# The factor of the norms: two products with a constant matrix and Exp of Ln, in place of one-column products, Sqrt and a transposed spread

## Chip, core and metric

The kernel runs on one core of a Trainium2 chip. The metric is the device time of one execution in microseconds (us). Engines: TensorE (PE, its weight loads PEld), VectorE (DVE), ScalarE (ACT), GpSimd (POOL), and SyncE (SP), which issues DMAs, as GpSimd does.

## The reference, cut to what matters

One decoder layer over 2048 tokens with 1024 channels, all in float32. Three sub-layers follow each other, each as x + RMSNorm(f(RMSNorm(x))):

```python
def rms_norm(x, g):
    y = x * lax.rsqrt(jnp.mean(x * x, axis=-1, keepdims=True) + EPS)
    return y * g
...
# 1. mixer: z = h @ w_in (a, g, q, k, v, forget logits)
#    u = silu(layer_norm(causal_conv31(a * sigmoid(g))))            512 channels
#    att = causal attention, 8 heads of 64, with cumulative log-forget bias
#    y = concat(u, att) @ w_out
# 2. cross-attention of 4 heads into 256 memory tokens (themselves normed)
# 3. y = square(relu(h @ w_up)) @ w_down                            hidden 4096
```

The layer norm over the 512 conv channels subtracts the mean and multiplies by rsqrt(mean of squares + EPS) as well.

## The kernel before

**Layout and precision.** Activations stand transposed: channels on the 128 partitions, tokens along the free dimension, in chunks of 512 tokens (TC), eight tiles of 128 channels (KT). A float32 product is made of three products in the f32r format: each operand is split into a high part (a ScalarE copy that rounds) and a low part (a VectorE subtraction), `split` (L134), and `mm3` (L160) adds high x high, high x low and low x high in PSUM.

**A norm.** `square_sum` (L169) squares the eight channel tiles on ScalarE and adds them on VectorE into one tile `ss` of 128 partitions x 512 tokens. `token_mean` (L177) turns each block of 128 tokens of `ss` by an f32 product with a one-column vector of 1/1024, so that the mean of a token lies on that token's partition, one column for each block. `token_rstd` (L185) applies Sqrt(mean + EPS) on ScalarE and a reciprocal on VectorE, on 128 x 4 elements. `spread` (L193) brings the factor back to a row over tokens on all partitions with one transpose on TensorE for each block, into the one PSUM bank of tag "stat", from which VectorE multiplies. So it is done in `normed` (L288: x, four chunks, and memory with 256 tokens), `conv_norm` (L455: four chunks, whose mean over channels is one f32 product with a broadcast column of ones, L463), `residual` (L650: behind the mixer and behind the cross-attention, four chunks each), `mlp_out` (L906: chunks 0 to 2) and `finale` (L863: chunk 3, in two halves of 256 tokens). Two further uses of `token_mean` need no spread: the norm ahead of the cross-attention (`mix_out`, L664, uses the factor as a scale per token) and the one ahead of the MLP (`mlp_prep`, L785).

**Stages and order.** `run` (L978): `mix_in` for the first half of the tokens with memory and the norms of the other two chunks beside it; `mix_in` for the second half, and the MLPs of chunks 0, 1 and 2, each with side work beside it (`tail`: for each chunk attention, `mix_out`, cross-attention); the MLP of chunk 3 alone; `finale`. `mlp_out(c)` runs beside the first five hidden blocks of the next chunk's MLP; `mlp_prep(c+1)` beside the last block of the MLP of chunk c. `drive` (L956) steps a main and a side generator in turn by the costs that they yield, side costs against main costs by a ratio (r0, a1, m0, m1, m2), and deals the conv taps out by another (a0, b1, bm). A planner then orders each engine's instructions by priority and by its own estimate of times; the other constants of SCHED (L57) shift priorities: weights are issued ahead by hw, conv taps behind by hb, side and main by hs and hm. While `Engine.pinned` is set (the first stretch of the kernel), each instruction of ScalarE and VectorE stays in the order of the program.

**Buffers.** Every tile has a tag with a number of buffers (L43 on): of [128 x 512] tiles "ms" has four for the main work (squares, relu, the reads `x2r` of the residual in `mlp_out`, `r2b` and `ssy` of the finale), "bs" three for the side work; in PSUM "mm" has two banks for main products, "stat" one.

**Tables.** ScalarE's functions come in table sets. A load (ACT_TABLE_LOAD) is put ahead of an activation whose function isn't in the set that is loaded; Square, Copy and Relu never need one.

Of the kernel before, what the change touches and what calls it, by code (L numbers as in the profile page):

```python
# [11 lines left out]
F32R = mybir.dt.float32r  # L12
AF = mybir.ActivationFunctionType
# [43 lines left out]
SCHED = dict(hw=153, hb=124, hs=61, hm=42.2, r0=0.254, a0=0.346, a1=1.16, b1=0.186, m0=0.85, m1=0.986, m2=1.12,  # L57
             bm=0.102, y1=3.12, y2=2.3, y3=2.97, y4=1.95)
# [22 lines left out]
class Trunk:  # L81
# [103 lines left out]
    def token_rstd(self, ss, mean):  # L185

        n = ss.shape[1] // P
        r = self.st([P, 4], name="rstd")[:, :n]
        self.a.activation(r, self.token_mean(ss, mean), AF.Sqrt, bias=self.eps, scale=1.0)
        self.v.reciprocal(r, r)  # L190
        return r

    def spread(self, r):  # L193

        n = r.shape[1]
        ps = self.ps("stat")
        for t in range(n):
            self.nc.tensor.transpose(ps[:, t * P : (t + 1) * P], r[:, t : t + 1].to_broadcast([P, P]), self.ident)
        return ps[:, : n * P]

# [11 lines left out]
    def setup(self):  # L212
# [6 lines left out]
        self.mean_d, self.mean_c = ct([P, 1], "mean_d"), ct([P, 1], "mean_c")  # L219
        self.v.memset(self.mean_d, 1.0 / D)  # L220
        self.v.memset(self.mean_c, 1.0 / CCH)
# [9 lines left out]

        self.tri = ct([P, P], "tri")
        self.same, self.prior = [ct([NH * 8, NH * 8], n) for n in ("same", "prior")]
# [14 lines left out]

    def setup_late(self):
# [12 lines left out]
        n = NH * 8  # L262
        sel = lambda t, pattern, base, cm: nc.gpsimd.affine_select(
            out=t, in_=t, pattern=pattern, compare_op=ALU.is_ge, fill=0.0, base=base, channel_multiplier=cm)
        for t in (self.tri, self.same, self.prior):
            nc.gpsimd.memset(t, 1.0)
        sel(self.tri, [[1, P]], 0, -1)
        sel(self.prior, [[1, n]], -1, -1)
        for t in (self.same, self.prior):
            t = t.rearrange("p (h t) -> p h t", t=8)  # L270
            sel(t, [[-8, NH], [0, 8]], 0, 1)
            sel(t, [[8, NH], [0, 8]], 7, -1)
# [15 lines left out]
    def normed(self, xs, g, w, stag, out=None, tags=None):  # L288
# [5 lines left out]
        r = self.token_rstd(ss, self.mean_d)  # L294
        yield 1
        r = self.spread(r)
# [50 lines left out]
    def mix_in(self, h, ht, late, after):  # L347
# [15 lines left out]
        for b in range(2):  # L363
# [32 lines left out]
    def glu(self, h, t, ht):  # L396
# [58 lines left out]
    def conv_norm(self, a, tag):  # L455
# [6 lines left out]
        mu = self.ps("stat")  # L462
        self.nc.tensor.matmul(mu, self.ones[:, 0:1].to_broadcast([P, P]), tot, start=True, stop=True)  # L463
        ss = self.tile(tag, [P, TC], name="lss")
        for t in range(4):
            self.v.scalar_tensor_tensor(out=a[:, t], in0=mu, scalar=-1.0 / CCH, in1=a[:, t],
# [3 lines left out]
        r = self.token_rstd(ss, self.mean_c)  # L470
        yield SCHED["y4"]
        r = self.spread(r)
        for t in range(4):
            self.mul(a[:, t], a[:, t], r)
            self.a.activation(a[:, t], a[:, t], AF.Silu, bias=self.cvec[:, 2, t : t + 1],
                              scale=self.cvec[:, 1, t : t + 1])
            yield SCHED["y4"]

    def gate(self, h, z):

        nc = self.nc
        z, e, u, ln, cum = z
# [18 lines left out]
        if h == 1:  # L501
            nc.tensor.matmul(ps[:n, :1], self.same, self.tot[0], start=True, stop=False)
        nc.tensor.matmul(ps[:n, :1], self.prior, self.tot[h], start=h == 0, stop=True)
# [146 lines left out]
    def residual(self, ys, ss, xs, dst):  # L650

        r = self.token_rstd(ss, self.mean_d)
        yield 1.5
        r = self.spread(r)
# [9 lines left out]
    def mix_out(self, c, g):  # L664
# [27 lines left out]
        yield from self.residual(ys, ss, xs, self.d_x1[c])  # L692
# [12 lines left out]
    def cross(self, c, h2, sc, g):  # L705
# [75 lines left out]
        yield from self.residual(ys, ss, xs, self.d_x2[c])  # L781
# [81 lines left out]
    def finale(self, c, cur, ys, r4):  # L863
# [8 lines left out]
        def out(sl, ssy):  # L872
            r = self.spread(self.token_rstd(ssy, self.mean_d))
# [32 lines left out]
    def mlp_out(self, c):  # L906
        nc = self.nc
        ys, ssy = self.fin.pop(c)
        r = self.spread(self.token_rstd(ssy, self.mean_d))
# [198 lines left out]
```

## Time and profile before

| | us |
|---|---|
| median of three runs | 2823.07 |
| lowest and highest | 2816.79, 2825.55 |
| profiled execution, its own time | 2820.59 |
| its span, first to last instruction | 2818.8 |
| TensorE busy | 2745.9 (97%) |
| VectorE busy | 1962.6 (70%) |
| ScalarE busy | 1372.1 (49%) |
| GpSimd busy | 206.1 (7%) |
| mean granted clock of TensorE, as a share | 0.995 |

How to read it: the median is what a change is measured by; the busy times and all rows below come from the one profiled execution. Register, branch, semaphore and DMA-issuing instructions are not counted as busy. Products on TensorE overlap in the records, so that their lengths add up to more than the time that they take.

### The profile page before, as it was taken

How to read it: one execution, taken by the hardware profiler on the slowest of the kernel's cores; microseconds unless marked ns; L12 is line 12 of the kernel's file. 1: busy time of each engine (PE TensorE's matmuls, PEld its weight loads, DVE VectorE, ACT ScalarE, POOL GpSimd, SP SyncE). 2: the span in 40 equal slices, each digit the busy share in tenths (PEclk: the TensorE clock that was granted, in tenths of full speed). 3: DMA queues.
4: the chain of work that ended last, by engine and by line, in shares of the span. 5: the costliest groups of instructions: out<-in, count | busy, mean ns of one | idle time of the engine just before them, and what ended most of it. 6: DMA issues, size and time to landing. Idle time of an engine off the chain costs nothing.

```text
span 2818.8 us, 36129 instructions
## 1 busy us (share of the span) xinstructions
PE 2745.9 (97%) x13300; PEld 2255.2 (80%) x13300; DVE 1962.6 (70%) x3596; ACT 1372.1 (49%) x2171; POOL 206.1 (7%) x376
## 2 busy tenths in 40 slices
PE   7999999999999999999999999999999999999997
PEld 5889778887877888777878888778777888888886
DVE  7677876668785666787885766997875555844436
ACT  5224644346654435465654444665555445543332
POOL 0010300001110000021100001021100000000000
PEclk9999999999999999999999999999999999999999
DMA  5375645456543334455543435464524342442222
GB/s 171 117 239 161 168 135 173 141 159 198 163 145 113 135 127 146 142 171 150 156 130 123 146 114 172 128 192 140 153 97 143 131 150 77 140 136 97 92 96 83
DMA packets 141169, 398.26 MB, mean 141 GB/s; under 512 B 15264, under 2 KB 38048, under 8 KB 136128
## 3 DMA queue, kind: packets, MB, share of 16 engines
q1 hardware_dynamic: 100080, 262.40, 28.3%
q0 software_dynamic: 40912, 133.54, 16.0%
q8 instruction: 105, 1.72, 0.3%
q14 instruction: 72, 0.59, 0.1%
HBM read 330.68 MB, written 65.20 MB: 140 GB/s over the span
## 4 chain that ended last, share of the span: by engine, by line
PE 87%; DMA 5%; DVE 4%; issue 2%; ACT 2%; POOL 0%; SPq 0%; DVEq 0%; POOLq 0%; ACTq 0%
PE mm L166 20%; PE mm L165 20%; PE mm L167 20%; PE sc L167 4%; PE sc L165 4%; PE sc L166 4%; PE o L631 4%; PE pt L613 4%; PE sc L578 2%; PE sc L579 2%; DMA rb<-drs 1%; DMA ks<-dk 1%; DVE yacc L73 1%; DMA x2r<-dx 1%; PE stat L182 1%
## 5 line engine op out<-in xcount | busy, mean ns | idle before, releaser
L73 ACT CAST wh<-wr 128x1024 fp32r<-128x1024 f32 x282 | 296.3, 1051 | 664.8 <-PE mm L166 602.0
L165 PE MATMUL mm<-h,wh 128*128 128x512 f32 x1504 | 597.7, 398 | 3.4 <-ACT h L73 2.6
L167 PE MATMUL mm<-h,wl 128*128 128x512 f32 x1504 | 595.0, 396 | 0.0
L166 PE MATMUL mm<-h,wh 128*128 128x512 f32 x1504 | 592.9, 394 | 1.8 <-DVE h L73 1.8
L73 DVE TENSOR_TENSOR wl<-wr,wh 128x1024 fp32r<-128x1024 f32 x282 | 345.0, 1224 | 278.0 <-ACT wh L73 276.6
L165 PE MATMUL mm<-hid,wh 128*128 128x512 f32 x992 | 397.6, 401 | 0.9 <-DVE yacc L73 0.9
L167 PE MATMUL mm<-hid,wl 128*128 128x512 f32 x992 | 395.6, 399 | 0.0
L166 PE MATMUL mm<-hid,wh 128*128 128x512 f32 x992 | 394.2, 398 | 0.0
L73 DVE SCALAR_TENSOR_TENSOR acc<-cu,convw,acc 128x512 f32<-128x512 f32 x480 | 357.6, 747 | 5.8
L165 PEld LDWEIGHTS mm<-h,wh 128*128 128x128 f32 x1504 | 283.4, 189 | 62.1 <-ACT h L73 3.0
L166 PEld LDWEIGHTS mm<-h,wh 128*128 128x128 f32 x1504 | 283.3, 188 | 59.8 <-DVE h L73 3.3
L167 PEld LDWEIGHTS mm<-h,wl 128*128 128x128 f32 x1504 | 283.0, 188 | 59.2 <-issue 0.5
L73 DVE TENSOR_TENSOR yacc<-mm,yacc 128x512 f32<-128x512 f32 (+1 forms) x232 | 154.7, 668 | 154.5 <-PE mm L167 153.6
L73 ACT CAST pp<-pt 128x512 fp32r<-128x512 f32 (+1 forms) x288 | 158.9, 561 | 135.5 <-PE pt L613 123.2
L165 PEld LDWEIGHTS mm<-hid,wh 128*128 128x128 f32 x992 | 186.5, 188 | 43.9 <-DVE yacc L73 2.2
L167 PEld LDWEIGHTS mm<-hid,wl 128*128 128x128 f32 x992 | 186.5, 188 | 41.9 <-issue 0.2
L166 PEld LDWEIGHTS mm<-hid,wh 128*128 128x128 f32 x992 | 186.6, 188 | 40.2 <-issue 0.2
L73 DVE TENSOR_TENSOR pp<-pt,pp 128x512 fp32r<-128x512 f32 (+1 forms) x288 | 185.8, 655 | 43.3 <-ACT pp L73 41.6
L613 PE MATMUL pt<-ident,prow 128*128 128x128 f32 x1088 | 195.1, 274 | 0.7 <-ACT prow L73 0.7
L73 DVE CUSTOM_DVE_ANT_0 prow<-sc,bias 128x512 f32<-128x512 f32 (+3 forms) x288 | 166.7, 595 | 24.6 <-PE sc L579 19.0
L73 ACT ACTIVATE prow<-prow,mx 128x128 f32<-128x128 f32 (+15 forms) x128 | 154.3, 1205 | 57.5 <-DVE mx L73 56.8
L613 PEld LDWEIGHTS pt<-ident,prow 128*128 128x128 f32 x1088 | 139.7, 141 | 33.0 <-ACT prow L73 3.9
(242 smaller groups left out, 4427.6 us busy)
## 6 DMA issues: line engine op xcount, KB each, us to landing
wr<-in_w_up_dram SPq DMA_DIRECT2D x128, 512.0 KB, 3.4
wr<-in_w_down_dram SPq DMA_DIRECT2D x128, 512.0 KB, 3.5
wr<-in_w_in_dram SPq DMA_DIRECT2D x32, 512.0 KB, 4.0
q<-dq POOLq DMA_DIRECT2D x64, 256.0 KB, 6.0
wr<-in_w_out_dram SPq DMA_DIRECT2D x32, 512.0 KB, 3.5
dx<-y SPq DMA_DIRECT2D x16, 1024.0 KB, 4.4
bias<-dnc POOLq DMA_DIRECT2D x32, 512.0 KB, 5.1
x<-in_x_dram POOLq DMA_DIRECT2D x12, 1024.0 KB, 6.2
```

Source lines behind the costliest of these rows:

```text
L73: ins = op(*args, **kw)
L165: mm(ps, ah, bh, start=first and j == 0, stop=False)
L166: mm(ps, ah, bl, start=False, stop=False)
L167: mm(ps, al, bh, start=False, stop=last and j == n - 1)
L182: self.nc.tensor.matmul(ps[:, t : t + 1], ss[:, t * P : (t + 1) * P], mean, start=True, stop=True)
L578: nc.tensor.matmul(ps[:, :w], q[:, 0, qs], ks[:, k0 : k0 + w], start=True, stop=False)
L579: nc.tensor.matmul(ps[:, :w], q[:, 1, qs], ks[:, k0 : k0 + w], start=False, stop=True)
L613: nc.tensor.transpose(pt[:, at : at + P], prow[t][:, (k0 + k) * P : (k0 + k + 1) * P], self.ident)
L631: nc.tensor.matmul(o[:, :, q], v[:, g + k], pp[:, :, at + q.start : at + q.stop], start=g == 0 and k == 0 and (n == 0 or nk == 2), stop=g ...
```

## The change

`wide_mean` splits the tile of sums into a high and a low part and multiplies both by one constant 128 x 128 matrix, every element 1/1024, in two f32r products: the mean of every token then lies on all partitions at once. `wide_rstd` takes Ln(mean x scale + EPS) and Exp of -0.5 times that on ScalarE, in place in the tile of sums, from which the multiplications read it; the spread is gone from `normed`, `conv_norm`, `residual`, `mlp_out` and `finale`. The conv norm's mean over channels goes through `wide_mean` as well, with a factor of two in the scalar, since the matrix holds 1/1024. `token_rstd`, left for the norm ahead of the cross-attention, takes Ln and Exp too. One table set is loaded by an instruction of its own (`ln_exp`) at the start, behind the second Sigmoid of each gated unit and behind the last Silu of a conv norm; each Sigmoid and Silu is kept behind the ScalarE instruction that was traced before it. The masks `same` and `prior` of the forget gate are made in the gate's own buffer before each half's value products, no longer once at the start. Of the constants of SCHED hw, hb, r0, m2, bm and y4 have new values. Code that isn't shown does not change.

```diff
-SCHED = dict(hw=153, hb=124, hs=61, hm=42.2, r0=0.254, a0=0.346, a1=1.16, b1=0.186, m0=0.85, m1=0.986, m2=1.12,
-             bm=0.102, y1=3.12, y2=2.3, y3=2.97, y4=1.95)
+SCHED = dict(hw=162, hb=117, hs=61, hm=42.2, r0=0.297, a0=0.346, a1=1.16, b1=0.186, m0=0.85, m1=0.986, m2=1.08,
+             bm=0.0831, y1=3.12, y2=2.3, y3=2.97, y4=2.07)
...
 def token_rstd(self, ss, mean):
-        self.a.activation(r, self.token_mean(ss, mean), AF.Sqrt, bias=self.eps, scale=1.0)
-        self.v.reciprocal(r, r)
+        self.a.activation(r, self.token_mean(ss, mean), AF.Ln, bias=self.eps, scale=1.0)
+        self.a.activation(r, r, AF.Exp, scale=-0.5)
...
+    def wide_mean(self, x, tag):
+        w = x.shape[1]
+        hi, lo = [self.tile(tag, [P, w], F32R, "wm") for _ in range(2)]
+        self.split(hi, lo, x)
+        ps = self.ps("stat")[:, :w]
+        self.nc.tensor.matmul(ps, self.wide, hi, start=True, stop=False)
+        self.nc.tensor.matmul(ps, self.wide, lo, start=False, stop=True)
+        return ps
+
+    def wide_rstd(self, ss, tag, n=D):
+        r = ss
+        ps = self.wide_mean(ss, tag)
+        self.a.activation(r, ps, AF.Ln, bias=self.eps, scale=float(D // n))
+        self.a.activation(r, r, AF.Exp, scale=-0.5)
+        return r
...
 # setup
+        self.wide = ct([P, P], "wide", F32R)
+        self.a.activation(self.wide, self.mean_d[:, 0:1].to_broadcast([P, P]), AF.Copy, scale=1.0)
-        self.a.activation(self.st([P, 1], name="warm"), self.eps, AF.Sqrt)
+        self.ln_exp()
...
 # normed
-        r = self.token_rstd(ss, self.mean_d)
+        r = self.wide_rstd(ss, stag)
         yield 1
-        r = self.spread(r)
         yield 1
...
 # mix_in, at b == 0
-                buf = self.tile("ms", [P, 4 * 8 * NH + P], name="gate")
+                buf = self.tile("ms", [P, 6 * 8 * NH + P], name="gate")
+                zs += [buf[: NH * 8, 384 + 64 * j : 448 + 64 * j] for j in range(2)]
+                self.gate_masks(*zs[5:])
...
 # glu
-            self.a.activation(sig, ps, AF.Sigmoid)
+            self.tc.keep_in_program_order(self.a.activation(sig, ps, AF.Sigmoid))
+            if j == 1:
+                self.ln_exp()
...
 # conv_norm
-        mu = self.ps("stat")
-        self.nc.tensor.matmul(mu, self.ones[:, 0:1].to_broadcast([P, P]), tot, start=True, stop=True)
+        mu = self.wide_mean(tot, tag)
...
-        r = self.token_rstd(ss, self.mean_c)
+        r = self.wide_rstd(ss, tag, CCH)
         yield SCHED["y4"]
-        r = self.spread(r)
         for t in range(4):
             self.mul(a[:, t], a[:, t], r)
-            self.a.activation(a[:, t], a[:, t], AF.Silu, bias=self.cvec[:, 2, t : t + 1],
-                              scale=self.cvec[:, 1, t : t + 1])
+            self.tc.keep_in_program_order(self.a.activation(
+                a[:, t], a[:, t], AF.Silu, bias=self.cvec[:, 2, t : t + 1], scale=self.cvec[:, 1, t : t + 1]))
+            if t == 3:
+                self.ln_exp()
...
 # residual
-        r = self.token_rstd(ss, self.mean_d)
+        r = self.wide_rstd(ss, tag)
         yield 1.5
-        r = self.spread(r)
         yield 1
...
 # finale and mlp_out
-            r = self.spread(self.token_rstd(ssy, self.mean_d))
+            r = self.wide_rstd(ssy, "ms")
```

## Rows read from the trace of the kernel before

**Rows 1.** The page: totals by engine, and its chain that ended last, by engine.

```profile
PE 2745.9 (97%) x13300; PEld 2255.2 (80%) x13300; DVE 1962.6 (70%) x3596; ACT 1372.1 (49%) x2171; POOL 206.1 (7%) x376
...
PE 87%; DMA 5%; DVE 4%; issue 2%; ACT 2%; POOL 0%; SPq 0%; DVEq 0%; POOLq 0%; ACTq 0%
```

**Rows 2.** Stretches: length, busy us (instructions) of each engine, clock, DMA share.

```profile
0.00:45.00 45.00, 26.11 (x108) 20.71 (x109) 32.31 (x49) 24.89 (x35) 6.15 (x21) 1.00 0.57 192
...
2460.00:2780.00 320.00, 320.00 (x1407) 262.65 (x1406) 135.51 (x153) 120.82 (x161) 2.69 (x5) 1.00 0.32 108
2780.00:2819.00 39.00, 24.39 (x195) 23.04 (x194) 30.31 (x82) 8.58 (x22) 0.00 (x0) 0.88 0.16 55
```

**Rows 3.** Timeline of TensorE in the first conv norm: start, length, instruction.

```profile
377.97 0.40 PE L166 MATMUL mm<-h,wh 128*128 128x512 f32 x1
378.20 0.95 PE L182 MATMUL stat<-mean_c,lss 128*128 128x1 f32 x8
...
379.33 0.40 PE L165 MATMUL mm<-h,wh 128*128 128x512 f32 x1
...
381.16 0.39 PE L167 MATMUL mm<-h,wl 128*128 128x512 f32 x1
381.38 0.60 PE L198 MATMUL stat<-ident,rstd 128*128 128x128 f32 x4
...
382.05 0.39 PE L166 MATMUL mm<-h,wh 128*128 128x512 f32 x1
```

**Rows 4.** Instructions on tile stat: count, ns min/median/max, first and last start.

```profile
L198 PE MATMUL stat<-ident,rstd x82: 270/272/448, 15.3 to 2809.5; 128*128 128x128 f32 x82
```

**Rows 5.** Timeline of TensorE at the third conv norm's mean.

```profile
1457.32 0.39 PE L166 MATMUL mm<-h,wh 128*128 128x512 f32 x1
1457.54 1.02 PE L463 MATMUL stat<-tot,ones 128*128 128x512 f32 x2
...
1458.63 0.39 PE L165 MATMUL mm<-hid,wh 128*128 128x512 f32 x1
```

**Rows 6.** Groups of ScalarE and VectorE: busy us, mean ns, idle before.

```profile
L73 ACT CAST hid<-relu 128x512 fp32r<-128x512 f32 x128 | 79.7, 622 | 2.5
...
L73 ACT ACT_TABLE_LOAD x49 | 62.9, 1283 | 19.0 <-DVE mmx L73 17.2 <-PEq L1097 0.8 <-DVE nss L73 0.2
L73 ACT ACTIVATE y<-sc,gains 128x512 f32<-128x512 f32 x64 | 43.8, 685 | 41.6 <-PE sc L167 41.4
...
L73 DVE TENSOR_TENSOR hid<-relu,hid 128x512 fp32r<-128x512 f32 x128 | 88.0, 689 | 49.9 <-ACT hid L73 49.8
...
L73 DVE TENSOR_TENSOR y<-y,stat 128x512 f32<-128x512 f32 x64 | 41.8, 679 | 8.7 <-PE stat L198 8.7
```

**Rows 7.** Timeline of ScalarE and VectorE at the end, in the finale.

```profile
2793.95 0.41 DVE L73 TENSOR_TENSOR ssy<-ssy,sq 128x256 f32<-128x256 f32 x1
...
2795.28 0.41 ACT L73 ACTIVATE ssy<-yacc 128x256 f32<-128x256 f32 x1
...
2807.61 0.41 DVE L73 TENSOR_TENSOR ssy<-ssy,sq 128x256 f32<-128x256 f32 x1
...
2809.77 0.87 DVE L73 SCALAR_TENSOR_TENSOR yacc<-yacc,gains,stat 128x256 f32<-128x256 f32 x2 [0.53 <-PE stat L198]
```

**Rows 8.** TensorE's waits: for whom, us in total, times, longest.

```profile
PE stat L497 <- DVE gate L73: 1.5, 1, 1.5
```

**Rows 9.** Timeline of the start.

```profile
13.23 1.22 DVE L73 TENSOR_TENSOR wl<-wr,wh 128x1024 fp32r<-128x1024 f32 x1 [0.48 <-ACT wh L73]
...
16.46 1.41 DVE L73 SCALAR_TENSOR_TENSOR x<-x,gains,stat 128x512 f32<-128x512 f32 x2 [1.27 <-PE stat L198]
...
32.87 0.60 ACT L73 ACTIVATE sig<-mm 128x512 f32<-128x512 f32 x1
...
34.94 1.03 ACT L73 CAST xh<-wr 128x1024 fp32r<-128x1024 f32 x1
```

**Rows 10.** The reads of the residual into x2r, from 1200 to 1300 us.

```profile
DMA to landing us min/median/max: 2.9/4.4/6.8
```

More of the change, by code (lines that the diff above doesn't have):

```diff
@@ L218, in setup @@
         self.v.memset(self.ones, 1.0)
-        self.mean_d, self.mean_c = ct([P, 1], "mean_d"), ct([P, 1], "mean_c")
+        self.mean_d = ct([P, 1], "mean_d")
         self.v.memset(self.mean_d, 1.0 / D)
-        self.v.memset(self.mean_c, 1.0 / CCH)
+        self.wide = ct([P, P], "wide", F32R)
+        self.a.activation(self.wide, self.mean_d[:, 0:1].to_broadcast([P, P]), AF.Copy, scale=1.0)
         self.eps = ct([P, 1], "eps")
         self.v.memset(self.eps, EPS)
-        self.a.activation(self.st([P, 1], name="warm"), self.eps, AF.Sqrt)
+        self.ln_exp()
         self.g = ct([P, 7, KT], "gains")
@@ L232, in setup @@
         self.tri = ct([P, P], "tri")
-        self.same, self.prior = [ct([NH * 8, NH * 8], n) for n in ("same", "prior")]
         self.rs = {c: ct([P, NH, 4], f"rs{c}") for c in range(NCH)}
@@ L247, in setup, with ln_exp @@
         self.d_x2 = [self.dram([P, KT, TC], name="dx2") for _ in range(NCH)]
+    def ln_exp(self):
+        ins = mybir.InstLoadActFuncSet(name=self.nc.get_next_instruction_name(), act_func_set_id=6,
+                                       engine=mybir.EngineType.Activation)
+        self.tc.keep_in_program_order(self.nc.scalar.add_instruction(ins))
     def setup_late(self):
@@ L261, in setup_late, with keep, gate_masks @@
         self.split(self.wf[:, 0], self.wf[:, 1], raw)
[L262 to L269, printed above, removed]
+        nc.gpsimd.memset(self.tri, 1.0)
+        self.keep(self.tri, [[1, P]], 0, -1)
+    def keep(self, t, pattern, base, channel):
+        self.nc.gpsimd.affine_select(out=t, in_=t, pattern=pattern, compare_op=ALU.is_ge, fill=0.0, base=base,
+                                     channel_multiplier=channel)
+    def gate_masks(self, same, prior):
+        for t in (same, prior):
+            self.nc.gpsimd.memset(t, 1.0)
+        self.keep(prior, [[1, NH * 8]], -1, -1)
+        for t in (same, prior):
             t = t.rearrange("p (h t) -> p h t", t=8)
-            sel(t, [[-8, NH], [0, 8]], 0, 1)
-            sel(t, [[8, NH], [0, 8]], 7, -1)
+            self.keep(t, [[-8, NH], [0, 8]], 0, 1)
+            self.keep(t, [[8, NH], [0, 8]], 7, -1)
     def mem_load(self):
@@ L461, in conv_norm @@
         yield SCHED["y4"]
-        mu = self.ps("stat")
-        self.nc.tensor.matmul(mu, self.ones[:, 0:1].to_broadcast([P, P]), tot, start=True, stop=True)
+        mu = self.wide_mean(tot, tag)
         ss = self.tile(tag, [P, TC], name="lss")
         for t in range(4):
-            self.v.scalar_tensor_tensor(out=a[:, t], in0=mu, scalar=-1.0 / CCH, in1=a[:, t],
+            self.v.scalar_tensor_tensor(out=a[:, t], in0=mu, scalar=-float(D // CCH), in1=a[:, t],
                                         op0=ALU.mult, op1=ALU.add)
@@ L481, in gate @@
         nc = self.nc
-        z, e, u, ln, cum = z
+        z, e, u, ln, cum, same, prior = z
         lt = ln.rearrange("p h t -> p t h")
@@ L501, in gate @@
         if h == 1:
-            nc.tensor.matmul(ps[:n, :1], self.same, self.tot[0], start=True, stop=False)
-        nc.tensor.matmul(ps[:n, :1], self.prior, self.tot[h], start=h == 0, stop=True)
+            nc.tensor.matmul(ps[:n, :1], same, self.tot[0], start=True, stop=False)
+        nc.tensor.matmul(ps[:n, :1], prior, self.tot[h], start=h == 0, stop=True)
         off = self.st([n, 1], name="off")
@@ L648, in take_y, with residual @@
         self.square_sum(ss, ps, f == 0, tag)
-    def residual(self, ys, ss, xs, dst):
-        r = self.token_rstd(ss, self.mean_d)
+    def residual(self, ys, ss, xs, dst, tag):
+        r = self.wide_rstd(ss, tag)
         yield 1.5
-        r = self.spread(r)
         yield 1
@@ L691, in mix_out @@
         xs = self.x_load(c, self.load, g["k"])
-        yield from self.residual(ys, ss, xs, self.d_x1[c])
+        yield from self.residual(ys, ss, xs, self.d_x1[c], g["s"])
         h2 = self.pair8(TC, "h2", [g["k"]] * 4)
@@ L780, in cross @@
                 yield 2.6
-        yield from self.residual(ys, ss, xs, self.d_x2[c])
+        yield from self.residual(ys, ss, xs, self.d_x2[c], g["s"])
         self.x2[c] = ys
@@ L908, in mlp_out @@
         ys, ssy = self.fin.pop(c)
-        r = self.spread(self.token_rstd(ssy, self.mean_d))
+        r = self.wide_rstd(ssy, "ms")
         yield 1
```

## The prediction

> **What bounds the kernel now.** I read the totals first: TensorE is busy 97% of the span, VectorE 70%, ScalarE 49%, GpSimd 7% [rows 1]. Then the chain that ended last: 87% of it is TensorE, 2% ScalarE [rows 1]. Then stretches: from 2460 to 2780 us TensorE is busy for all 320 us [rows 2]. The reader is to see that the kernel is one long queue of products and that time is won by shortening that queue, while work on other engines counts only where TensorE waits for it: at the start, at the very end, and in a few short gaps.
>
> In this queue what an instruction costs is the step from its start to the next start, not its listed length: in that full stretch 1407 instructions, nearly all products of 512 columns, share 320 us, 0.227 us each [rows 2].
>
> **The change, part by part.** The profiled execution took 2820.59 us (span 2818.8); the median of the runs is 2823.07. I work from the former.
>
> 1. *The factor on TensorE.* Before, a norm over 512 tokens queues eight one-column products (four blocks, two passes each) and later four transposes. From the product at 377.97 to the one at 379.33 are 1.36 us, in which two ordinary products run as well; less 2 x 0.227 the eight cost 0.90 us. From 381.16 to 382.05 are 0.89 us, again with two products: the transposes cost 0.44 us [rows 3]. Together 1.34. After, there are two f32r products of 512 columns, 0.454 us: 0.89 less per norm. How many: 82 transposes of a norm's factor are listed [rows 4], so 82 blocks of 128 tokens, that is 19 norms of 512 tokens and three of 256 (memory, and the two halves of the finale). The first two norms of x and the second half of the finale don't lie in the stream and come below. So 17 x 0.89 = 15.1 us, and for the two of 256 half of it each, 2 x 0.44 = 0.9 us.
>
> 2. *The mean in the conv norm.* It is an f32 product of 512 columns in two passes: from 1457.32 to 1458.63 are 1.31 us with two ordinary products in them, so it costs 0.86 us [rows 5]. After: 0.454. Four times 0.4 = 1.6 us.
>
> So the queue loses 15.1 + 0.9 + 1.6 = 17.6 us.
>
> 3. *ScalarE and VectorE.* Added per norm and per mean of 512 columns: a copy (nearest row 0.62) and a subtraction (0.69); for norms also Ln (nearest row with a per-partition operand 0.69) and Exp (0.62) [rows 6]. On VectorE that is 23 x 0.69 and some 1.3 for the three small ones, 17 us, against small reciprocals gone; on ScalarE 23 x 0.62 + 19 x 1.31 and some 4, 43 us, against 22 small square roots gone. Of the 49 table loads of 1.28 us [rows 6] I keep about 31 (one at the start, one or two ways to Sigmoid and as many back in each of eight gated units, two in each of four conv norms: 25 to 41), so 23 us go. Net some 15 us more on either engine, taken as 0 on the path, hidden by the 97% of TensorE. If that cover is gone it is paid in the chain of a norm: bare, it took 1.75 us from the end of the last sum of squares to the first use (2808.02 to 2809.77) [rows 7]; after, 0.62 + 0.69 + 0.4 + 0.69 + 0.62 and hand-offs, some 3.4. That is +1.6 us per norm where TensorE has no other work, at most 23 x 1.6 = 37 us; and below nothing, to -1.28, where a table load stood in that chain.
>  The factor is now read from SBUF and not from PSUM. The multiplication with a PSUM operand took 679 ns, the nearest with two SBUF operands 689 [rows 6]: 0. [...]
>
> 4. *Gate.* Abs, Exp and Ln need no load in between any more. TensorE stood 1.5 us once for the gate's VectorE result [rows 8]; a load of 1.28 lies in that result's chain. I take -1.5 us (bounds 0 and -3, two gates).
>
> 5. *Masks.* Two fills and five selections leave the start and run on GpSimd before each half's gate instead, ahead of loads of the side work in its queue. A GpSimd instruction takes 0.55 us on average [rows 1], so 4 us of queue twice. GpSimd is 7% busy and loads are issued well ahead: 0, at most 8.
>
> 6. *Start.* Here TensorE waits for the norm. First norm: VectorE is at a weight's low part until 14.45, so the subtraction ends at 15.1; the last product at 15.6, Ln at 16.3, Exp at 17.0; before, the first use was at 16.46 [rows 9]. +0.6. Second norm: the Sigmoid ends at 33.47 [rows 9], the copy at 34.1, the table load at 35.4 (subtraction and products beside it), Ln at 36.1, Exp at 36.8; the next weight's cast, kept in program order behind it, began at 34.94 [rows 9] and TensorE waits for that weight. +2.0. Together +2.6; bounds 0 (the second half of x is needed only later) and +3.9 (Exp wants yet another load).
>
> 7. *End.* The last norm is bare: before 1.75 us [rows 7]; after, with 256 columns, 0.42 + 0.42 + 0.3 + 0.45 + 0.42 and five hand-offs of 0.1, 2.5 us: +0.8. The first half's norm wants two more "ms" buffers beside r2b, its own sum and the second half's sum: five of four. If the second half's sum comes ahead, the split waits until r2b is free, at the end of all products, and the first half's sixteen VectorE instructions come behind: eight pairs of at most 0.87 us [rows 7], up to +7. The first half's sum ends at 2794.4, so its copy ends at 2794.8 and the low part takes its buffer then; the second half's first square began at 2795.28 [rows 7]. The split is ahead by 0.4 us, so I take 0.
>
> 8. *The constants of the interleaving.* No row shows the new order. TensorE idles 73 us of the span [rows 1], of these 18.9 in the first 45 us and 14.6 in the last 39 [rows 2]. The other 40 us are what a new order could give back or double: I take 0, and 15 us either way for the range.
>
> Sum: -17.6 - 1.5 + 2.6 + 0.8 = -15.7, so 2820.6 - 15.7 = 2804.9, taken as 2805. The median stands 2.5 us above the profiled run, so a measured median may come out at 2803 to 2808.
>
> **The rivals.**
> *A, slower: relu waits for a buffer.* In an MLP of chunks 1 to 3 the first five hidden blocks run beside the output of the chunk before. There the factor now stays in one of four "ms" buffers for all eight outputs (before it was in PSUM), and the reads of the residual (x2r) take others. A read lands after 2.9 to 6.8 us [rows 10]. If a freed buffer goes to the next read ahead of relu, relu waits for a read and two VectorE instructions of 0.69, 5.8 us at the median of 4.4 and 8.2 at most; the second "mm" bank covers one block of 24 x 0.227 = 5.4 us. From the point where the wait is over 5.4, TensorE stands: up to 2.8 us in each of 15 blocks, 42 us; at three quarters of that, 2805 + 33 = 2838. For it: the split's two buffers fall into the same stretch. Against it: reads come in pairs, which leaves relu one buffer, and it needs just one.
> *B, the gain is given back.* Sigmoid and Silu are now kept behind whatever ScalarE instruction was traced before them, an attention Exp with its wait included, while they hold one of two "mm" banks or the side's turn; and the longer chain (+1.6) meets TensorE in conv norms and residuals. Half of 16 such places at 1.6 us is 13 us: 2818, no change. For it: ScalarE is idle half the time, so the order of its queue is not free of waits. Against it: beside the side work there is always main work.
> *C, more than that:* the new constants give back 15 of the 40 us: 2790.
> *D, it doesn't do what it says:* Ln and Exp come from different sets, so that each of 22 norms has two loads, 56 us of ScalarE; where the chain is bare (start and end, 2.6 us each, and a few stalls) that costs some 7 us: 2812. For it: the load placed by hand stands only behind the second Sigmoid and the last Silu, so norms in between are left to an automatic choice. [...]
>
> **How the numbers follow.** Forecast, 2798 to 2812: 0.50; C 0.17; B 0.17; D 0.07; A 0.09. A measurement of this kernel tells no change within 0.3%, 8.5 us: faster means under 2814.6, slower over 2831.5. Faster: nearly all of the forecast, C and D, 0.71. Same: B and the edges of the others, 0.19. Slower: A and a little of B, 0.10. The range holds the forecast, D, most of C and B: 2786 to 2824; A and the tails, 2 in 10, are left out.
>
> **What would show it.** Right: some 200 TensorE instructions fewer (82 x 3 and 8 gone, 2 x 26 added), its queue shorter by 17 us with gaps as before; about 31 table loads; x first used near 17.0; no PSUM operand in multiplications by the factor. Wrong: TensorE idle well above 73 us; relu waiting for readers of x2r after 1240, 1850 and 2460; a first-half norm of the finale that begins behind the last product; 60 or more table loads.

## The result, and the profile after

The changed kernel took 2842.76 us (median of 4 runs, 2840.02 to 2849.98) against 2821.92 for the kernel before on the same chip: ratio 1.0079, interval 1.0054 to 1.0104. It is slower by 21 us; the prediction said faster by 16. The profiled execution took 2849.98 us, span 2848.3, the longest of the four.

The page of the changed kernel, totals and chain; they answer to [rows 1].

```profile
PE 2746.2 (96%) x13098; PEld 2245.0 (79%) x13098; DVE 1975.2 (69%) x3595; ACT 1392.6 (49%) x2212; POOL 210.8 (7%) x383
...
PE 61%; DMA 4%; DVE 3%; issue 2%; ACT 1%; POOL 0%; DVEq 0%; POOLq 0%; ACTq 0%
```

TensorE has 202 instructions fewer, the number forecast, and is busy as long as before: its time outside work went from 73 to 102 us, and part of its work ran slower. The queue itself did shrink. TensorE's timeline at a norm in the stream (start, length, instruction) answers to [rows 3]:

```profile
1591.00 0.39 PE L165 MATMUL mm<-h,wh 128*128 128x512 f32 x1
1591.23 0.39 PE L207 MATMUL stat<-wm,wide 128*128 128x512 f32 x1
1591.46 0.39 PE L166 MATMUL mm<-h,wh 128*128 128x512 f32 x1
1591.69 0.40 PE L167 MATMUL mm<-h,wl 128*128 128x512 f32 x1
1591.93 0.39 PE L208 MATMUL stat<-wm,wide 128*128 128x512 f32 x1
1592.16 0.40 PE L165 MATMUL mm<-h,wh 128*128 128x512 f32 x1
```

Two products of a norm cost 0.23 + 0.23 us, as ordinary ones do. Without the losses counted below, TensorE's time from its first product to its last fell from 2724.6 to 2709.3 us. So most of the 17.6 us of the prediction's sum are there, and some 39 us (17.6 and 21) were lost elsewhere. Stretches of the changed kernel (length, busy us of each engine, granted clock, DMA share) show where:

```profile
0.00:45.00 45.00, 20.79 (x63) 14.38 (x64) 29.13 (x43) 29.42 (x39) 4.89 (x14) 0.93 0.53 179
388.00:404.00 16.00, 7.41 (x19) 5.20 (x18) 14.82 (x18) 11.07 (x10) 0.00 (x0) 0.68 0.15 49
660.00:674.00 14.00, 6.40 (x31) 5.38 (x29) 12.29 (x34) 6.53 (x13) 1.61 (x3) 0.63 0.50 160
1487.00:1500.00 13.00, 7.05 (x20) 5.23 (x19) 7.57 (x8) 4.00 (x6) 0.00 (x0) 0.74 0.28 85
2460.00:2780.00 320.00, 317.89 (x1385) 259.95 (x1384) 141.83 (x168) 122.81 (x165) 4.31 (x8) 0.99 0.33 107
2780.00:2848.00 68.00, 46.58 (x291) 41.12 (x290) 41.80 (x92) 20.08 (x38) 0.00 (x0) 0.88 0.21 70
```

The full stretch is nearly as full as in [rows 2]; the loss sits in a few places, and at each of them the granted clock is low too (0.63 to 0.93). The kernel before, at the place of the second line, has

```profile
388.00:404.00 16.00, 16.00 (x70) 12.53 (x69) 14.19 (x16) 6.85 (x7) 0.00 (x0) 1.00 0.23 82
```

TensorE's waits in the changed kernel (for whom: us in total, times, longest):

```profile
PE stat L207 <- ACT wm L73: 23.6, 5, 13.7
PE sc L165 <- ACT cat L73: 9.2, 2, 7.5
PE mm L165 <- DVE yacc L73: 8.3, 6, 5.9
PE stat L182 <- DVE ss L73: 7.6, 1, 7.6
```

The 13.7 us of the first line are the time ahead of TensorE's first product (12.8 in the kernel before). The other long waits are the first conv norm (7.5), the third (5.9) and the norm ahead of the first MLP (7.6, at 661 us).

**The clock behind a stall.** In the first conv norm TensorE stands for 7.5 us and then goes on at half pace: its steps are 0.43 us and not 0.23 (granted clock 0.50 from 396.3 to 404.0), until 403.9.

```profile
388.40 0.39 PE L167 MATMUL mm<-h,wl 128*128 128x512 f32 x1
396.26 0.79 PE L165 MATMUL sc<-cat,xh 128*128 128x512 f32 x1 [7.48 <-ACT cat L73]
...
399.62 0.63 PE L165 MATMUL sc<-cat,xh 128*128 128x512 f32 x1
400.04 0.63 PE L166 MATMUL sc<-cat,xh 128*128 128x512 f32 x1
```

In the whole run the granted clock is 0.50 for 82 us, 30 in the kernel before; 65 and 20 of these lie ahead of the last product. So this stall is paid twice, once while it lasts and once behind it; the prediction priced only the first.

**Loss by place.** The time of TensorE is counted in steps, from the start of one instruction to the start of the next. A step that is over 0.3 us longer than the median of its kind counts as a wait, with what it has above that median; for other steps that start at a granted clock of 0.50, what they have above the median is added. In us, by stretches of each kernel's own span (the places shift by some 15 us at most): 0-200 is the start, 370-420 the first conv norm, 600-680 the norm ahead of the first MLP, 1200-1310 the turn of the first chunk, 1450-1510 the third conv norm; the last stretch holds the second and fourth conv norm and the end of the third MLP. The two columns on the right go from the first product to the last one of the last MLP: all losses, and the rest of that time.

```
                           0-200 200-370 370-420 600-680 1200-1310 1450-1510 820-890+2060-2520   all    rest
before                       8.6   14.5     0.4     9.1     13.5       1.3           6.3        66.7  2724.6
after                       16.6   11.3    12.2    11.3     10.2      10.2          16.2       102.7  2709.3
e1  before, new constants    8.2   12.1     1.1    11.2      3.3       8.6           8.6        66.2  2727.6
e10 before, Ln and Exp      11.2   15.2     1.5    10.1      8.6       1.3           7.9        70.4  2727.8
e13 before, order kept       8.2   14.0     6.9     9.2     10.8       1.3           5.8        68.8  2725.6
e9  after, all norms small  10.1   16.3     7.4    11.4      8.1      14.9           5.0        84.6  2725.7
e2  after, old constants    15.9   15.2    11.3     9.7     16.8       6.9          10.9        97.5  2710.4
e3  after, end's buffers    16.5   14.1    10.8    11.2      6.7       9.5          14.5        97.6  2709.5
e5  e3, order free          15.8   11.7     2.5    12.4     10.2       7.6          12.5        89.1  2713.6
e6  e3, conv norm small     16.4   11.6     5.4    12.1     10.7      15.8          10.2        96.1  2711.6
e8  e3, first norms small   10.8   12.6    10.5    12.3      6.7       9.3          17.7        89.6  2716.9
e15 wide in the stream       8.2   15.8     0.4     9.6     17.8       1.3           5.4        72.6  2714.1
e16 residuals wide only      8.2   13.1     0.4    10.2     10.1       0.9           2.7        64.5  2720.5
```

Each row is one execution. The steps at a granted clock of 0.50 that are not counted as waits cost 19.5 us in the changed kernel and 7.8 in the kernel before.

### The profile page after: what moved, and what is told of

It is laid out like the page before. It is cut to its first block, busy times and chain, and to the rows that moved or that the text cites. A ratio compares the mean times of both kernels' runs of the same rounds, so it can differ in the third digit from the quotient of the medians.

```text
span 2848.3 us, 35777 instructions
## 1 busy us (share of the span) xinstructions
PE 2746.2 (96%) x13098; PEld 2245.0 (79%) x13098; DVE 1975.2 (69%) x3595; ACT 1392.6 (49%) x2212; POOL 210.8 (7%) x383
## 3 DMA queue, kind: packets, MB, share of 16 engines
q0 software_dynamic: 40912, 133.54, 16.3%
## 4 chain that ended last, share of the span: by engine, by line
PE 61%; DMA 4%; DVE 3%; issue 2%; ACT 1%; POOL 0%; DVEq 0%; POOLq 0%; ACTq 0%
PE mm L165 14%; PE mm L166 14%; PE mm L167 14%; PE sc L167 3%; PE sc L165 3%; PE sc L166 3%; PE o L666 3%; PE pt L648 3%; PE sc L613 2%; PE sc L614 1%; DMA x2r<-dx 1%; DMA wr<-in_w_out_dram 1%; DVE yacc L73 1%; DMA ks<-dk 1%; DVE wl L73 1%
## 5 line engine op out<-in xcount | busy, mean ns | idle before, releaser
L165 PEld LDWEIGHTS mm<-hid,wh 128*128 128x128 f32 x992 | 187.6, 189 | 52.8 <-DVE yacc L73 10.8
```

The lines of the kernel that those rows point to most:

```text
L165: mm(ps, ah, bh, start=first and j == 0, stop=False)
```

## The experiments

All 18 are timed against the kernel before on the same chip. A ratio with its interval is that of the means to the kernel before; the times in us are medians.

```
after                1.0079 (1.0054-1.0104)
e1  1.0014 (1.0001-1.0028)  e2  1.0082 (1.0064-1.0100)  e3  1.0055 (1.0040-1.0069)
e4  1.0092 (1.0075-1.0110)  e5  1.0034 (1.0018-1.0050)  e6  1.0063 (1.0041-1.0085)
e7  1.0087 (1.0064-1.0110)  e8  1.0067 (1.0046-1.0088)  e9  1.0050 (1.0035-1.0064)
e10 1.0026 (1.0016-1.0036)  e11 1.0022 (1.0013-1.0032)  e12 1.0032 (1.0022-1.0042)
e13 1.0012 (1.0004-1.0021)  e14 1.0058 (1.0045-1.0072)  e15 0.9994 (0.9984-1.0004)
e16 0.9987 (0.9977-0.9998)  e17 1.0032 (1.0020-1.0044)  e18 1.0047 (1.0030-1.0063)
```

**The constants alone (e1) and the old ones on the change (e2).** `SCHED` exchanged (six values), nothing else.

> The kernel before with nothing changed but the seven new constants of the interleaving (norms as they were). If the new order is itself what costs (it sets norms and loads where TensorE has nothing else), this kernel is slower than the one before by a good part of the 21 us, 8 us or more. If the constants were found for the new norms and do them good, and the loss lies in the norms, it may be either side of the kernel before, and old constants on the new norms are then worse than the new ones. My own term (0, 15 either way) holds if it lies within 5 us.

> The changed kernel with the old constants of the interleaving. If the loss is the order: the queue's 17 us come out, less about 8 at the end and 5 at the start, so some 2815, faster than before. If the loss is the longer chain of a norm wherever it meets TensorE: still over 2830, with stalls at other places than 388, 661 and 1488 us, TensorE at half its clock for some tens of us behind them.

e1 took 2825.92, +3 us: my own term (0, within 5 us) holds, the theory of the order does not, and whether the constants were found for the new norms stays open (with the old ones the change is 2 us slower, within the intervals). e2 took 2844.96, over 2830 as the theory of the longer chain has it; but the stall at the first conv norm stays (11.3 us lost there), so the places are not those that it forecast. On the kernel before the new constants move loss: in e1 the turn of the first chunk loses 3.3 us in place of 13.5, and the third conv norm 8.6 in place of 1.3.

**The end's buffers (e3).**

```diff
-            r = self.wide_rstd(ssy, "ms")
+            r = self.wide_rstd(ssy, "bs")
```

> The changed kernel with the split of the last chunk's two norms (256 columns each) put into buffers of the side's tag, long idle by then, and no longer into the four that the sums, squares and the factor of the MLP share. Theory: the low part of the first half waited for the MLP factor's buffer until all products were done (2827.13), and the first half's sixteen VectorE instructions and the second half's squares came behind it. Then the first half's output runs beside the second half's products, and from the last product to the end of the span it takes about 15 us and not 22.5: -7 us. Rival: the VectorE work of the end is as long in either order, and the end stays within 2 us of 22.5.

2836.63, 6 us below the changed kernel by the medians; from the start of the last MLP product to the end of the span 16.3 us and not 22.4 (14.6 before). The theory holds. ScalarE and VectorE at the end of the changed kernel, against [rows 7]:

```profile
2817.04 0.42 ACT L73 ACTIVATE ssy<-yacc 128x256 f32<-128x256 f32 x1 [1.02 <-DVE yacc L73]
2817.36 0.39 ACT L73 CAST wm<-ssy 128x256 fp32r<-128x256 f32 x1
...
2826.60 0.42 DVE L73 TENSOR_TENSOR yacc<-yacc,r2b 128x256 f32<-128x256 f32 x1
2827.13 0.42 DVE L73 TENSOR_TENSOR wm<-ssy,wm 128x256 fp32r<-128x256 f32 x1
...
2829.18 0.87 DVE L73 SCALAR_TENSOR_TENSOR yacc<-yacc,gains,ssy 128x256 f32<-128x256 f32 x2
```

The second half's sum takes its buffer at 2817.04, just ahead of the split's copy, so the low part is the fifth user of four buffers and starts when the last multiplication by r2b is done, 9.8 us later. In e3 it follows its copy at once:

```profile
2810.78 0.41 ACT L73 CAST wm<-ssy 128x256 fp32r<-128x256 f32 x1 [0.62 <-DVE ssy L73]
...
2811.22 0.43 DVE L73 TENSOR_TENSOR wm<-ssy,wm 128x256 fp32r<-128x256 f32 x1
```

**The set behind every Sigmoid (e4).**

```diff
-            if j == 1:
-                self.ln_exp()
+            self.ln_exp()
```

> The changed kernel with the set of Ln and Exp loaded by hand behind every Sigmoid, and not only behind the second of a gated unit. Theory: the norms that fall between two Sigmoids (start 34.86 and 37.15 us, first conv norm 381 and 384, first residual 475 and 477) lose their two loads of 1.28 us each: first use of the second norm at the start about 2 us earlier, the stall at 388 us shorter by 2.5 or more and with it less time at half the clock, about -5 to -8 us in all; some 8 loads more on ScalarE cost nothing. Rival: loads move, but the stalls are set by other waits (VectorE's multiplication by rb, the order of casts), and the time stays within 2 us.

2848.12, no faster than the changed kernel: the theory falls. The stall of the first conv norm is 6.1 us there (7.5 in the changed kernel), and the first product with the second norm of x is at 40.0 (40.1): the loads moved, most of the waits stayed.

**Parts of e3 put back (e5 to e8).** e5 takes `keep_in_program_order` off Sigmoid and Silu; e6 gives the conv norm, e7 the residuals, e8 the norms of x and the memory the old form (Ln and Exp stay, on the small tile), as here in e7:

```diff
-        r = self.wide_rstd(ss, tag)
+        r = self.token_rstd(ss, self.mean_d)
         yield 1.5
+        r = self.spread(r)
```

> As e3_finale_buffers (the changed kernel with the end's buffers mended, 2836.6 us), and Sigmoid and Silu no longer kept behind the ScalarE instruction traced before them (the load of the set of Ln and Exp still stands right behind the second Sigmoid and the last Silu). Theory of the pins: Sigmoid and Silu wait behind other work while they hold a bank or the side's turn, and the kernel gains 5 us or more, to 2832 or less. Theory of the chain: the order of these instructions is not what TensorE waits for; within 3 us of e3, with the stalls at 390, 661 and 1482 us as they are, perhaps more table loads than 38.

> As e3_finale_buffers, with the conv norm's mean by one product with the column of ones and its factor on 128x4 numbers with a spread, as before (Ln and Exp stay in place of root and reciprocal, on the small tile). Theory of the chain: the copy, the subtraction and the two functions on 512 columns, 3.4 us and in the queues of busy engines, come twice in each conv norm, and behind them stand the stalls at 390 (6.4 us), 874 (1.5), 1482 (6.3) and 2138 to 2161 us (4.2) of e3, 18 us with more at half the clock; this kernel then loses 5 us of the queue's gain and wins back 15 or more: 2827 or less. Theory of the loads of tables or of the order: the stalls stay, and the kernel is 0 to 5 us slower than e3.

> As e3_finale_buffers, with the eight norms of the two residuals on 128x4 numbers with a spread, as before (Ln and Exp on the small tile). The queue's gain of 8 x 0.89 = 7 us is lost. Theory: the residual's chain is beside main work nearly always; of the stalls only the one at 661 us (7.8 in e3, 5.0 in the kernel before) hangs on it, so the kernel ends 2 to 6 us slower than e3. Rival: the longer chain of the residual puts the whole side work late and so sets the later stalls too: 2832 or less.

> As e3_finale_buffers, with the norms of x and of the memory on 128x4 numbers with a spread, as before (Ln and Exp on the small tile). Theory: in the first 45 us TensorE has no other work; the second norm's first use goes from 40 back to 36 or 37 us and with it some 3 us at half the clock; the three norms in the stream lose 2 us of the queue: 2832 to 2835. Rival: what is won in the first 45 us is waited for later anyway: within 1 us of e3.

e5 2833.29, e6 2839.07, e7 2846.03, e8 2838.99, against 2836.63 for e3.

e5 gains 3 us, less than the theory of the pins asked for, but at the first conv norm it shows the cause: that place loses 2.5 us in place of 10.8. ScalarE there in the changed kernel:

```profile
390.07 2.93 ACT L73 ACTIVATE cu<-cu,cvec 128x512 f32<-128x512 f32 x4 [2.29 <-DVE cu L73]
...
394.31 1.90 ACT L73 CAST cat<-cu 128x2048 fp32r<-128x2048 f32 x1
...
397.52 0.60 ACT L73 ACTIVATE sig<-mm 128x512 f32<-128x512 f32 x1
```

By 388.8 TensorE has filled both banks of main products. The Sigmoid that would free one is kept behind four Silus (in e3 too, at 398.28), and TensorE's next main product, at 398.17, waits for it. In e5 the Sigmoid goes ahead of the Silus, and TensorE works on at full clock (its line, and the stretch as above):

```profile
388.60 0.60 ACT L73 ACTIVATE sig<-mm 128x512 f32<-128x512 f32 x1
...
388.00:404.00 16.00, 15.89 (x71) 12.59 (x70) 14.39 (x18) 12.31 (x12) 0.00 (x0) 1.00 0.15 50
```

e6 and e8 refute my theories of the time: their own stalls shrink (370 to 420 us: 5.4 in e6 after 10.8; the start 10.8 in e8 after 16.5), the time does not. In e6 the turn and the third conv norm lose more (10.7 us after 6.7, 15.8 after 9.5). In e8 the losses fall by 8 us in all and the rest grows by 7, of which the norms' products explain 4; why the remainder grows is open. e7 shows that the wide norm does pay in the residuals: without it the kernel is 9 us slower, no less than its 7 us of queue.

**All norms small (e9).** e6, e7, e8 and the finale and outputs put back together.

> The changed kernel with every norm on 128x4 numbers and a spread, and the conv norm's mean by the column of ones, as before. What is left of the change: Ln and Exp on the small tile in place of root and reciprocal, the set loaded by hand, Sigmoid and Silu kept in order, the masks and the new constants. Theory 1 (the wide norms themselves cost: gap by gap more than their 17 us on TensorE): the time is near the kernel before, 2822 to 2828. Theory 2 (the kept order of Sigmoid and Silu, the loads and the constants cost, and the wide norms do bring their 17 us): the queue's gain is gone and the stalls stay, 2845 or more.

2838.43. With TensorE's old queue the kernel is 15 us slower than before, and e3, with all the wide norms, is the same within the intervals: the wide norms' 17.6 us of queue and what they cost elsewhere cancel. The other parts cost some 15 us.

**These parts one by one on the kernel before (e10, e13; e1 above).** e10 has Ln and Exp in `token_rstd` for Sqrt and reciprocal and the load by hand; e13 only the kept order.

> The kernel before with nothing changed but root and reciprocal of the small factor, which become Ln and Exp on 128x4 numbers, and the set of both loaded by hand behind the second Sigmoid of a gated unit and the last Silu. Theory of the sets: a norm that stands between two Sigmoids loads two sets, and both functions stand in ScalarE's queue behind its casts, where the reciprocal stood in VectorE's; slower by 5 us or more. Theory of the kept order: within 4 us of the kernel before, with fewer loads than its 49.

> The kernel before with nothing changed but that Sigmoid and Silu are kept behind the ScalarE instruction traced before them. Theory of the kept order: this alone puts the stall at the first conv norm (380 to 400 us) and costs 5 us or more. Theory of the sets or of sums of small things: within 4 us of the kernel before.

e10 2828.54 (+6), e13 2824.28 (+2), e1 +3: 11 to 12 us of e9's 15, if parts may be added. The rest I did not isolate. In e13 the kept order alone puts the stall at the first conv norm (6.9 us after 0.4), as its first theory has it, but most is won back elsewhere. In e10 no one place shows the 6 us: 2.6 lie in the first 50 us, and the rest is 3.2 longer (3.0 in e1); what Ln and Exp do and what the loads by hand do is not told apart.

**Mended kernels (e11, e12, e14, e18).** e11 joins e3 and e5 with the small form for the first two norms of x and the last half of the finale; e12 sets the wide norm's instructions earlier in priority; e14 has the old constants; e18 keeps Ln and Exp to the wide norms, with

```diff
         self.split(hi, lo, x)
+        if load:
+            self.ln_exp()
```

(`load` is set for the norms, not for the conv norm's mean over channels) in place of the loads behind Sigmoid and Silu, and root and reciprocal in the small ones.

> The changed kernel with four things mended together: the split of the finale in the side's buffers, Sigmoid and Silu not kept in order, and the three norms that stand bare (the first two of x, the last half of the finale) on the small tile with a spread. By the sum of what single edits moved (e5 against e3: -3; the start in e8: -5 of the gaps, with -4 at half the clock; the end 1.4): 2822 to 2828, the same as before. A kernel that beats the one before would show that nothing else stands in the way of the queue's gain; 2830 or more that the waits in the middle (661 and 1480 us) grow back.

> As e11_mended, with the instructions of the wide means and factors given an earlier place in the queues (150 steps of priority). If what the wide norm costs is its wait behind other work on ScalarE and VectorE (casts that wait for a weight's load stand in front of it), the stalls at 660 and 1480 us shrink and the kernel is 4 us or more below e11. If the chain's own length is what costs, within 2 us of e11.

> As e11_mended, with the old constants of the interleaving. If the new constants are what puts the stall at the third conv norm (8.6 us of gaps and half clock in e1, 1.3 in the kernel before), it goes and the kernel is 5 us or more below e11, 2823 or less. If the longer chain puts it there by itself (e2 had 6.9 at this place with the old constants), within 3 us of e11.

> As e11_mended (2828.8), but Ln and Exp only where the norm is wide, their set loaded by hand behind the copy of each wide norm and no longer behind Sigmoid and Silu; the small norms keep root and reciprocal; new constants, conv norm wide. If Ln and Exp on the small tile and the place of the loads cost here what they cost on the kernel before (6 us in e10), 2823. If that cost came only with the old order of the side work, within 2 us of e11.

e11 2828.75, e12 2831.37, e14 2836.73, e18 2832.19. None beats the kernel before, and e11 ends just over the 2822 to 2828 that its parts added up to. e12 is not faster than e11: an earlier place in the queues won nothing. e14 against e11: here the new constants are worth some 8 us, while on the kernel before they cost 3; neither theory of e14 had that. In e18 taking Ln and Exp from the small norms won nothing, but its table loads rose from e11's 38 to 52 with it; so it does not settle where e10's 6 us come from.

**What pays (e15, e16, e17).** e15 and e16 are the kernel before (old constants, root, free order) with the wide norm and the load of e18 in 13 norms of 512 tokens, the memory's and the finale's first half, or in the eight residuals alone; the masks are made as in the changed kernel. e17 is e15 with the new constants.

> Only the part of the change that the other runs found to pay: the wide norm in the residuals, in the outputs of the MLP chunks, in the norms of x 2 and 3 and of the memory, and in the first half of the finale (with the side's buffers), each with the set of Ln and Exp loaded by hand right behind its copy, beside the subtraction and the products. The conv norm, the first two norms and the last half keep the spread, root and reciprocal; old constants; Sigmoid and Silu free. Theory: 13 norms of 512 and two of 256 shorten TensorE's queue by 13 x 0.89 + 0.9 = 12.5 us and no chain that stands bare is longer: 2810 to 2814, faster than the kernel before. Rival: the side's chain is longer by 1.6 us at each of eight residuals and its work is waited for at 660 us and at the turns of chunks: 2818 to 2826.

> As e15_wide_in_stream, with the new constants of the interleaving. On the kernel before the new constants took 10 us of gaps and half clock from the turn of the first chunk (1200 to 1310 us) and put 7 at the third conv norm. If the same comes here, the time is within 3 us of e15 (2820). If the new constants suit the wide norms even where the conv norm stays small, 2815 or less, and the kernel beats the one before.

> As e15_wide_in_stream, with the wide norm in the eight residuals alone; the outputs of the chunks, the norms of x and of the memory and both halves of the finale keep the spread and root. Of the queue's 12.5 us 7.1 are left. If the residuals stand beside other work and the rest of e15's norms gave their gain back at 200 to 350 us (14.3 of gaps against 11.4 before) and at the turn of the first chunk (17.8 with the half clock against 13.5), the time is 2813 to 2817, the first kernel that beats the one before. If each wide norm gives back what it saves wherever it stands, 2820 to 2824.

e15 2820.17, not to be told from before: 10 us of queue are won and 6 us of losses added, 4.3 of them at the turn of the first chunk (17.8 us after 13.5), as the rival has it. e17 2830.44: the new constants cost 10 us here, outside both of its theories. e16 2819.42 against 2824.27, ratio 0.9987, its interval ending at 0.9998: of the 19 ratios the only one whose interval lies below 1, and barely, by some 4 us of its 7 us of queue. It can't be told from e15, and the kernel before took 2822.51 beside e1 to e4 on the same chip.

## Why the prediction was wrong

*Steps 1 and 2 (queue) held:* -202 instructions, 0.46 us per wide norm.

*Step 3 is the one that failed.* It took the longer chains of the wide norms as hidden "by the 97% of TensorE", with a bound of 37 us if that cover were gone. e3 and e9 differ by the wide norms and take the same time within the intervals, though e3's queue is 16 us shorter (rest 2709.5 against 2725.7): what the wide norms cost elsewhere is about what they save, some 17 us. Of these 13 are in the table (all losses 97.6 against 84.6): 6.4 at the start, 3.4 at the first conv norm and 9.5 at the second, the fourth and the end of the third MLP, while the third conv norm loses 5.4 less. The 97% are a mean over the span; they don't say that TensorE has other work at the moment a chain ends.

The whole miss adds up roughly: -17.6 of queue, +17 for what the wide norms cost elsewhere, +6 for the end's buffer (step 7), +15 for what e9 keeps (the order, Ln and Exp with their loads, the constants), which the prediction had at 0: +20, where +21 was measured. Each term is a difference of two kernels.

Not every stall is the chain's. At the first conv norm the kept order is enough (e13: 6.9 us with small norms; e5: 2.5 us with wide ones and the order free). At the third the new constants are enough. In the changed kernel a weight's cast stands in ScalarE's queue ahead of two squares and waits for its load; VectorE's sums wait for the squares, and the accumulation that TensorE needs stands among the sums. ScalarE there:

```profile
1484.14 0.63 ACT L73 ACTIVATE sq<-cu 128x512 f32<-128x512 f32 x1
1489.44 1.04 ACT L73 CAST xh<-wr 128x1024 fp32r<-128x1024 f32 x1 [4.66 <-DMA wr<-in_w_out_dram]
...
1491.33 1.14 ACT L73 ACTIVATE sq<-cu 128x512 f32<-128x512 f32 x2
```

VectorE at the same place:

```profile
1492.79 0.69 DVE L73 TENSOR_TENSOR lss<-lss,sq 128x512 f32<-128x512 f32 x1
1493.39 0.68 DVE L73 TENSOR_TENSOR yacc<-mm,yacc 128x512 f32<-128x512 f32 x1
```

TensorE stands for 5.9 us there. In e1, which has the new constants and no wide norm, the same cast waits nearly as long, with the squares ahead of it:

```profile
1470.26 1.05 ACT L73 CAST xh<-wr 128x1024 fp32r<-128x1024 f32 x1 [4.42 <-DMA wr<-in_w_out_dram]
```

The place loses 8.6 us in e1, 9.3 in e17, where the conv norm is small too, and 14.9 in e9. With the old constants and the wide conv norm it loses 6.2 in e14 and 6.9 in e2, with both old 1.3. So either change costs here, and they don't add.

*The operand (3):* the 0 held. The multiplication by the factor took 686 ns from SBUF, after 679 with a PSUM operand:

```profile
L73 DVE TENSOR_TENSOR y<-y,ss 128x512 f32<-128x512 f32 x64 | 42.0, 686 | 7.0 <-ACT ss L73 7.0
```

*Table loads (3 and rival D).* There are 38, not 31: 13 by hand (L273) and 25 placed automatically. The first of these stands ahead of the copy that makes the constant matrix (0.81 us), while of the 49 loads of the kernel before none has a square, a copy or a relu as the next instruction. The groups of ScalarE (count, busy us, mean ns, idle before):

```profile
L73 ACT ACT_TABLE_LOAD x25 | 32.1, 1283 | 1.4 <-PEq L1131 0.8 <-DVE nss L73 0.2
...
L273 ACT ACT_TABLE_LOAD x13 | 16.7, 1283 | 0.2
```

D is true of three norms (34.86 and 37.15 us, 381.36 and 384.55, 475.16 and 477.16), those that stand behind the first Sigmoid of a unit; here ScalarE at the second norm of x:

```profile
34.23 0.61 ACT L73 CAST wm<-nss 128x512 fp32r<-128x512 f32 x1
34.86 1.28 ACT L73 ACT_TABLE_LOAD   x1
36.44 0.69 ACT L73 ACTIVATE nss<-stat,eps 128x512 f32<-128x512 f32 x1 [0.30 <-PE stat L208]
37.15 1.28 ACT L73 ACT_TABLE_LOAD   x1
38.44 0.63 ACT L73 ACTIVATE nss<-nss 128x512 f32<-128x512 f32 x1
38.98 1.03 ACT L73 CAST xh<-wr 128x1024 fp32r<-128x1024 f32 x1
```

At each of these three norms the trace shows two loads, one ahead of Ln and one ahead of Exp (here 34.86 and 37.15). Behind a load by hand there is none between them: from the one at 543.83 to the next load at 858.31 stand a residual's Ln and Exp (637.58 and 638.42). So the automatic choice for Ln was not the set that is loaded by hand. The load at 37.15 takes 1.28 us, and the next function starts 0.01 us behind its end (38.44).

*Step 6 (start)* took +2.6 with a bound of 3.9; it was +0.8 for the first norm (x first used at 17.30, not 16.46) and +4.0 for the second (the cast at 38.98, not 34.94 [rows 9]), 4.8 together and some 3 us at half clock behind it (granted clock 0.50 from 41.0 to 45.5). The load between Ln and Exp that it left to its bound came.

*Step 7 (end)* named the fifth buffer and took it as 0, since the copy was ahead by 0.4 us in the trace of before. In the changed kernel's order of the queue that lead was gone: the end is longer by 7.8 us (22.4 after 14.6), of which e3 takes back 6.1.

*Step 4 (gate):* the loads went (253.81 and 256.59 at the first gate before, none from 204.71 to 291.86 now), the wait stayed, 1.0 us at 266 (1.5 before). *Step 5 (masks):* nothing seen, and e15 and e16 have the new masks without being slower. *Step 8 (constants)* was 0 with 15 either way: +3 on the kernel before, -8 (e11 against e14) and +10 (e17 against e15) on others.

*Rival A* appeared once and in another form: at 2500 us VectorE stood 3.75 us for a read of x2r, a weight's low part behind it, TensorE 2.0 us. *B* had the right mechanism (kept order, longer chains): 13 us, where the runs show some 17 for the wide norms and 2 for the order (e13); without the end, the constants and e10's 6 us it could not reach +21.

One sum of the prediction is off and bears on nothing else: three quarters of A's 42 us are 31.5 and not 33.

What stays open: the 6 us of e10, which have no single place, the last 3 us of e9, and how the 17 us split between the chain's length and the order that it changes.

## What to carry to other kernels

Work taken from the busiest engine pays only where the chain that replaces it doesn't end in front of that engine's queue. In this kernel the wide norm paid in the residuals, which stand beside other work (e7, and barely e16); that it is best left out at starts, ends and turns fits the losses by place, but e8 shows that a stall taken away in one place need not shorten the time. Where an order was tuned to a kernel, constants and chains change together, so a new part has to be timed with both orders before it is judged. Before an instruction is kept in its place in a queue, look at what stands ahead of it there and who waits for it (the Sigmoid behind four Silus). When a new tile joins a shared set of buffers, count the users at the tightest moment and give it another set if the count is one too many.

## What the hardware showed

In 106 runs of the kernel before, the mean granted clock of the span goes with its length: 2817.6 us on average in the 27 runs at 0.995, 2822.4 in 28 at 0.993, 2826.8 in two at 0.991, some 2.3 us for each 0.001. The changed kernel's four runs are at 0.9885 on average, the kernel before's mostly at 0.994: by that rate about 12 of the 22 us between their spans go with the lower clock, an estimate from these runs. The count of steps agrees: those at a granted clock of 0.50 cost 19.5 us in the changed kernel's trace and 7.8 in that of the kernel before.
